# A hybrid attention encoder on one core: TensorE's queue written out in program order, with projections, scores and V products paced by TensorE time

## The chip, the cores and the metric

The program runs on one core of a Trainium2 chip. The metric is the device time of one execution in microseconds, the median over the runs; lower is better. The core has TensorE (matrix products into PSUM), VectorE, ScalarE, GpSimd, and the queue of SyncE, from which nearly all DMAs are issued. In rows they are PE (PEld is its weight loads), DVE, ACT, POOL and SP.

## What is computed

One layer of an encoder with two mixers, for a prompt of 2048 positions and a sample of 512, with the same weights:

```
h = rmsnorm(x, g_pre) * (1 + scale) + shift            # shift, scale, gate = Linear(silu(c))
qa, ka, va, ga, qb, kb, vb, gb = split(h @ w_in)       # 1024 -> 4096; rope on q and k
ya = dilated_mixture(qa, ka, va) * silu(ga)            # 8 heads, windows (128,1), (512,4), (2048,16)
yb = diff_attention(qb, kb, vb, lam, g_sub) * silu(gb) # 4 heads: (softmax_1 - lam * softmax_2) @ v, dense
x  = x + gate * rmsnorm(concat(ya, yb) @ w_out, g_post)
```

All products are made of fp16 pairs: a value is a high part plus a low part, and a product is three matrix products (high by high, high by low, low by high), summed in PSUM.

## The kernel before

The work is cut into eight groups of columns: four of B (one head each, g = 4 to 7) and four of A (two heads each, g = 0 to 3), taken in the order 4, 0, 5, 1, 6, 2, 7, 3. The rows are cut into five blocks of 512: four of the prompt (p, c = 0 to 3) and the sample (s). The loop runs over the groups and, in each, over the blocks. One turn of it has **attention** of this group and block (`items`) and **projections** for what comes next (`qg_proj`: Q and gate of the next block; `kv_proj`: K and V of the same block for the next group), and from the last group on also the **output projection** (`out_proj`).

An item of B (`ItemB`, 128 rows, two maps m = 0 and 1) makes scores in halves of 1024 columns: two matmuls at L615 and two at L621, the latter on 64 rows of the array. VectorE scales each half in place and takes its row minimum (L624), ScalarE makes the exponentials (L636), VectorE joins the two maps (L655), ScalarE and GpSimd split the result (L657, L665), DMA transposes bring it to the layout of the V product, and 48 matmuls at L679 make it (`tail2`). At j = 3 four transposes (L704) and an evacuation end a block. An item of A (`ItemA`, 32 positions of each of four residues) has eight matmuls of 32 columns of the array at L738 and eight at L744, two reductions at L751 and L753, an exponential (L758), a split (L772, L774), transposes by DMA, and for four items together V products at L793 and L799.

The attention is a software pipeline in `run_items`: while item n makes scores, the one before it is split (`tail1`) and an earlier one has its V product (`tail2`, `tail3`). The V product of B is made two items later, at the point "late", behind the second map; that of A at "mid", three items later (`p3`).

PSUM in the loop: three places "sc" of 1024 columns for scores, one place "pj" of 512 for projections, one "pv" for V products, the transposes of B and `gate_half`. K/V (L472, evacuated by L478, L487 and L488), Q (L546, L553) and gate (L569, L573, L574) all go through "pj".

What sets the order: the loop emits attention and projections interleaved by `interleave`, and the framework's scheduler then puts every engine's instructions in the order of a simulated run, by readiness and priority (`high_priority` puts an instruction earlier). So TensorE's queue follows the simulated run and not the text. Side work (weight scaling in `raw_scale` with a maximum that goes through DRAM, `allmax_slow`, L194; splitting of weights, gates of the output) is woven in between (`weave`). When the last group has finished a block, `y_scale` makes the scale for that block through `allmax_slow`, and only then can `y_first` load and split it for the output projection (L946).

## Time and profile before

| | |
|---|---|
| median of 3 runs | 2251.14 us (2244.3 to 2253.18) |
| profiled execution | 2248.76 us, of which the instructions span 2247.0 us |
| TensorE busy | 1924.8 us (86%), 18506 matmuls |
| VectorE busy | 1421.3 us (63%) |
| ScalarE busy | 1159.5 us (52%) |
| GpSimd busy | 727.7 us (32%) |
| mean granted TensorE clock | 0.936 of full speed |
| DMA | 360.99 MB, 71.4% of the 16 engines' time on the main queue |

The stages in what follows are called B0, A0, B1, A1, B2, A2, B3, A3 in the order of the groups; a stage is the stretch from its first score matmul to that of the next group. Before B0 lie 170.3 us of opening, behind A3's last V product the rest of the output projection. A row of a group of instructions has the line, engine, operation, what it writes and reads, shapes and count, then busy time and mean duration of one, then the engine's idle time before them with what ended it. In a row of the timeline, the start and the duration come first, and idle time before it stands in brackets. Matmuls overlap, so what one costs is read from start to start.

### The profile page before, as it was taken

Reading aid. Unit: us, or ns where it says so; the run is one execution under the profiler, and the core shown is the slowest. Engines: PE = TensorE matmul, PEld = TensorE weight load, DVE = VectorE, ACT = ScalarE, POOL = GpSimd, SP = SyncE. Lnnn points to the kernel's source line nnn. Section 1 sums busy time; section 2 is a strip of 40 time slices with the busy share of each in tenths; the row PEclk is TensorE's granted clock in tenths of the full one; section 3 lists DMA queues with packets and bytes.
Section 4 is the critical chain, followed back from the end, with each engine's and each line's share of the span. In section 5 each row is a group of like instructions: output and inputs, shape, how many; then the busy total and the mean of one; then the engine's idle time right before and its main releaser. Section 6 shows DMA issues by size and latency. Waiting matters only on the chain. (4 is left out here: it accounts for less than half of the span.)

```text
span 2247.0 us, 47773 instructions
## 1 busy us (share of the span) xinstructions
PE 1924.8 (86%) x18506; PEld 1283.8 (57%) x18506; DVE 1421.3 (63%) x3224; ACT 1159.5 (52%) x2361; POOL 727.7 (32%) x1299
## 2 busy tenths in 40 slices
PE   4788997889799978988799878987789886999998
PEld 2565665566656655766466556764556654444443
DVE  3766776755677876665677857666567745454543
ACT  4556675644457655544467646454466643333321
POOL 1234654411146653111266451112445530110000
PEclk7899999999999989999799989998889998999999
DMA  7585877879777887887378778789676769465453
GB/s 301 165 254 141 161 176 142 168 140 190 153 157 147 156 179 152 164 158 166 91 148 162 157 187 152 154 175 250 127 161 133 167 154 182 110 126 125 120 164 113
DMA packets 727667, 360.99 MB, mean 161 GB/s; under 512 B 640432, under 2 KB 687296, under 8 KB 723984
## 3 DMA queue, kind: packets, MB, share of 16 engines
q1 hardware_dynamic: 726608, 357.08, 71.4%
q8 instruction: 145, 2.38, 0.5%
q0 software_dynamic: 832, 0.86, 0.5%
q14 instruction: 82, 0.67, 0.1%
HBM read 165.64 MB, written 36.98 MB: 90 GB/s over the span
## 5 line engine op out<-in xcount | busy, mean ns | idle before, releaser
L472 PE MATMUL pj<-w,h 128*128 128x256 f16 x3840 | 481.7, 282 | 66.9 <-DVE Vs L488 27.3
L472 PEld LDWEIGHTS <-h 128*128 128x128 f16 x3840 | 378.4, 101 | 149.5 <-issue 83.0
L665 POOL TENSOR_TENSOR hl<-pp,hl 128x1024 f16<-128x1024 f32 (+1 forms) x144 | 291.8, 2043 | 109.4 <-ACT hl L657 105.8
L546 PE MATMUL pj<-w,h 128*128 128x128 f16 x3840 | 265.2, 224 | 20.0 <-ACT q L553 8.6
L455 POOL TENSOR_TENSOR rp<-q,tab_sb 128x64 f32<-128x64 f32 x160 | 64.3, 402 | 635.1 <-ACT q L478 375.3
L546 PEld LDWEIGHTS <-h 128*128 128x128 f16 x3840 | 231.3, 100 | 58.3 <-issue 49.0
L624 DVE TENSOR_SCALAR_CACHE_REDUCE sc<-sc,us 128x1024 f32<-128x1024 f32 (+1 forms) x160 | 188.4, 1179 | 75.3 <-PE sc L621 74.8
L569 PE MATMUL pj<-h,w 128*128 128x512 f16 x960 | 223.4, 386 | 12.6 <-ACT q L553 12.6
L615 PE MATMUL sc<-K,Qc 128*128 128x512 f16 x512 | 162.6, 399 | 76.0 <-ACT pp L636 67.0
L679 PEld LDWEIGHTS <-at 128*128 128x128 f16 x3264 | 199.2, 102 | 35.9 <-issue 19.8
L774 DVE SCALAR_TENSOR_TENSOR hl<-pp,Z,hl 128x640 f16<-128x640 f32 (+2 forms) x160 | 140.9, 886 | 112.9 <-DMA at<-hl 63.4
L624 DVE TENSOR_SCALAR_CACHE_REDUCE sc<-sc,us,nb 128x1024 f32<-128x1024 f32 x128 | 172.4, 1347 | 57.0 <-PE sc L621 38.2
L679 PE MATMUL pv<-V,at 128*128 128x128 f16 x3072 | 198.8, 227 | 9.5 <-DMA at<-hl 8.2
L636 ACT ACTIVATE pp<-sc,nb 128x1024 f32<-128x1024 f32 (+1 forms) x144 | 152.5, 1062 | 85.9 <-DVE sc L624 55.2
L758 ACT ACTIVATE pp<-pp,nb 128x640 f32<-128x640 f32 (+2 forms) x160 | 131.5, 822 | 125.2 <-DVE nb L753 116.0
L772 ACT ACTIVATE hl<-pp,Z 128x640 f16<-128x640 f32 (+2 forms) x160 | 129.6, 821 | 109.0 <-DMA at<-hl 89.1
L655 DVE SCALAR_TENSOR_TENSOR pp<-pp,rz,pp 128x1024 f32<-128x1024 f32 (+1 forms) x144 | 172.3, 1233 | 1.8
L657 ACT ACTIVATE hl<-pp 128x1024 f16<-128x1024 f32 (+1 forms) x144 | 141.5, 1002 | 46.0 <-DVE pp L655 43.6
L569 PEld LDWEIGHTS <-w 128*128 128x128 f16 x960 | 92.9, 99 | 125.5 <-issue 27.0
L946 PEld LDWEIGHTS <-w 128*128 128x128 f16 x960 | 92.5, 98 | 115.0 <-issue 13.7
L636 ACT ACTIVATE pp<-sc,nbs 128x1024 f32<-128x1024 f32 (+1 forms) x144 | 152.5, 1061 | 10.3 <-DVE pp L655 6.1
L751 DVE CUSTOM_DVE_ANT_0 pp<-sc,maskp,us 128x384 f32<-128x384 f32 (+1 forms) x128 | 85.8, 679 | 77.6 <-PE sc L744 77.3
(210 smaller groups left out, 3085.6 us busy)
## 6 DMA issues: line engine op xcount, KB each, us to landing
h<-hp SPq DMA_DIRECT2D x124, 512.0 KB, 6.3
pp<-in_x_p_dram SPq DMA_DIRECT2D x32, 512.0 KB, 5.3
raw<-in_w_in_dram SPq DMA_DIRECT2D x8, 2048.0 KB, 8.3
h<-hs SPq DMA_DIRECT2D x32, 512.0 KB, 6.2
out_dram<-pp SPq DMA_DIRECT2D x20, 512.0 KB, 3.0
at<-hl SPq DMA_TRANSPOSE x608, 3.2
hp<-h SPq DMA_DIRECT2D x4, 2048.0 KB, 12.4
yp<-yt SPq DMA_DIRECT2D x32, 256.0 KB, 2.8
```

The source lines that it names most:

```text
L472: mm(ps[:, jj, :], lhsT=hT[:, a, k, j * P:(j + 1) * P], rhs=w[:, k, b, :], start=(k == 0 and i == 0), stop=(k == KT - 1 and i == 2))
L546: mm(ps[:, jj, 0:128], lhsT=hT[:, a, k, j * P:(j + 1) * P], rhs=w[:, k, b, 0:128], start=(k == 0 and i == 0), stop=(k == KT - 1 and i == 2))
L569: mm(ps, lhsT=w[:, k, b, 128:256], rhs=hT[:, a, k, :], start=(k == 0 and i == 0), stop=(k == KT - 1 and i == 2))
L615: mm(ps[:, n * 512:(n + 1) * 512], lhsT=Qc[:, j, m, 0, :], rhs=K[:, t:t + 4, m, :], start=True, stop=False)
L624: V.tensor_scalar(ps[:, :HW], ps[:, :HW], u["nsc"], nb[:, 0:1] if hf else 3e38, op0=ALU.mult, op1=ALU.min, accum_out=nb[:, hf:hf + 1])
L636: act(pt[m, hf][:, :HW], pss[hf][:, :HW], AF.Exp, scale=-1.0, bias=nbs, accum_out=Z[:, 2 * m + hf:2 * m + hf + 1])
L655: V.scalar_tensor_tensor(a, a, rz[:, 1:2], pt[0, hf][:, :HW], op0=ALU.mult, op1=ALU.add)
L657: act(hi[:, :HW], a, AF.Copy)
L665: nc.gpsimd.tensor_tensor(lo[:, :HW], a, hi, op=ALU.subtract)
L679: mm(po[:, :128], lhsT=a[:, k, :], rhs=Vv[:, k, 128 * b:128 * b + 128], start=(k == 0 and i == 0), stop=(k == NT - 1 and i == 2))
L758: act(sb[:, :NA], sb[:, :NA], AF.Exp, scale=-1.0, bias=nb[:, 1:2], accum_out=Z[:, 0:1])
L774: V.scalar_tensor_tensor(lo[:, :NA], sb[:, :NA], rz, hi[:, :NA], op0=ALU.mult, op1=ALU.subtract)
```

## The change

- **Program order.** The loop runs under `manual_schedule` for TensorE: its queue takes the matmuls as the text emits them. The other engines are scheduled as before; evacuations and reductions that free a PSUM place get `high_priority(offset=EARLY)`, EARLY = 150.
- **Pacing.** `pace` takes the place of `interleave`: the fill (projections) goes on when its TensorE time is not above its share of the attention's, plus a lead that shrinks to none; all costs (`yield 0.75` and so on) are TensorE times. While there is one "pj" alone, a projection begins only after 3.0 us of attention since the last ended (GAP).
- **Places.** `proj_bank` lets projections alternate between "pj" and a score place in all A groups and in the sample's block, and once at a group's start. Transposes at the end of a B block and `gate_half` go to a score place too.
- **V products.** Those of B are halved: 24 matmuls at "mid", between the two maps, the rest at "late". Those of A come one item later (`p4`).
- **Output projection.** Its share in the last group's block 1 falls from 20 to 8 (OPC).

```diff
-LEAD = [0, 0, 0, 0]
-OPC = [0, 20, 24, 24, 30]
+LEAD = [1.0, 6.0]
+GAP = 3.0
+EARLY = 150
+OPC = [0, 8, 24, 24, 30]
...
+    def proj_bank():
+        t = BANK["last"] = "sc" if (BANK["turns"] or BANK["once"]) and BANK["last"] == "pj" else "pj"
+        BANK["once"] = False
+        return PT([P, PS["w"]], t)[:, 0:512] if t == "sc" else PT([P, 512], t)
...
-            ps = PT([P, 2, 256], "pj")
+            ps = proj_bank().rearrange("p (a b) -> p a b", a=2)
...
-            act(k32.rearrange("p a b d -> p a (b d)"), ps[:, :, 0:128], AF.Copy, scale=2.0 ** -19)
+            with tc.high_priority(offset=EARLY):
+                act(k32.rearrange("p a b d -> p a (b d)"), ps[:, :, 0:128], AF.Copy, scale=2.0 ** -19)
...
                     if k % 4 == 3:
-                        yield 0.23
+                        yield "half" if i == 1 and k == NT // 2 - 1 else 0.27
...
-                pt_ = PT([P, 4, P], "pv")
+                pt_ = PT([P, PS["w"]], "sc")[:, 0:512].rearrange("p (a b) -> p a b", a=4)
...
-            yield 0.53 * Cc / 512
+            yield 0.93 * Cc / 512
...
-            yield 0.22
+            yield 0.75
...
                 if x == "mid":
-                    for q in (p3, p2):
-                        if isinstance(q, ItemA) and not q.done and (q is p3 or not isinstance(it, ItemA)):
-                            yield from q.tail2(getattr(it, "last", None))
+                    for q in (p4, p3, p2):
+                        if isinstance(q, ItemA) and not q.done and (q is p4 or not isinstance(it, ItemA)):
+                            yield from q.tail2()
...
+                    if isinstance(p2, ItemB):
+                        rest = p2.tail2()
+                        for y in rest:
+                            if y == "half":
+                                yield 0.27
+                                break
+                            yield y
                 elif x == "late":
+                    yield from rest
                     if isinstance(p3, ItemB):
                         yield from p3.tail3()
-                    if isinstance(p2, ItemB):
-                        yield from p2.tail2(getattr(it, "last", None))
...
+    def pace(main, mcost, fill, fcost, lead):
+        m = f = 0.0
+        start = True
+        while main is not None or fill is not None:
+            wait = start and BANK["gap"] and not BANK["once"] and PACE["since"] < GAP
+            if fill is not None and not (wait and main is not None) and                     (main is None or f <= fcost * m / mcost + lead * max(0.0, 1.0 - m / mcost)):
+                x = next(fill, None)
...
-    for n, g in enumerate(ORDER):
+    with tc.manual_schedule(engines={mybir.EngineType.PE}):
+        for n, g in enumerate(ORDER):
...
+                BANK["turns"] = n + 1 < NU and (g < 4 or r == "s")
+                BANK["once"] = n + 1 < NU and i == 0
+                BANK["gap"] = n + 1 < NU and not BANK["turns"]
+                pace(main, mc, weave(chain(*fl), side, 5 if side.__name__ == "raw_split" else 2), fc, LEAD[i == 0])
```

The order of TensorE's queue moves in three places that matter here. In the first, an A group (A0, block 1), the scores of several items stood together before; the rows leave out the weight loads and the repeats of a row (sc is the score tile, K and Qc what it is made of, w, h and pj a projection, at and pv a V product):

```order
L738 MATMUL sc_6774<-K_1783,Qc_6049 32x512
...
L744 MATMUL sc_6774<-K_1783,Qc_6049 32x256
...
L738 MATMUL sc_6847<-K_1783,Qc_6049 32x512
...
L744 MATMUL sc_6847<-K_1783,Qc_6049 32x256
...
L793 MATMUL pv_6892<-at,V_1786 128x128
...
L472 MATMUL pj_6564<-w_3269,h_5397 128x256
```

The same stage now, block 1 (L760 was L738, L766 was L744, L561 was L546):

```order
L561 MATMUL sc_6043<-w_1574,h_5399 128x128
...
L760 MATMUL sc_6068<-K_1785,Qc_5410 32x512
...
L561 MATMUL sc_6043<-w_1574,h_5399 128x128
...
L766 MATMUL sc_6068<-K_1785,Qc_5410 32x256
...
L561 MATMUL sc_6043<-w_1574,h_5399 128x128
...
L760 MATMUL sc_6125<-K_1785,Qc_5410 32x512
```

Each run of eight score matmuls now stands by itself between pieces of projections, and the projections also write into score places. Counted over TensorE's queue, it passes from the 32-column matmuls to others or back 93, 63, 63 and 505 times in A0 to A3 before, and 153, 153, 153 and 141 times now.

The second place is A3, where before nearly every score matmul stood alone between others, with its weight load (block 2):

```order
L738 LDWEIGHTS Qc_26646
L738 MATMUL sc_27290<-K_22374,Qc_26646 32x512
L546 LDWEIGHTS h_26632
L546 MATMUL pj_27300<-w_21759,h_26632 128x128
L738 LDWEIGHTS Qc_26646
L738 MATMUL sc_27290<-K_22374,Qc_26646 32x512
```

In A3 now, from the end of block 0's V products to the first matmul of the output projection (L976, L946 before):

```order
L821 MATMUL pv_26883<-at,V_3927_26051 128x4x32
...
L585 MATMUL pj_26864<-h_26101,w_21797 128x512
...
L760 MATMUL sc_26967<-K_22376,Qc_26106 32x512
...
L766 MATMUL sc_26967<-K_22376,Qc_26106 32x256
...
L760 MATMUL sc_27004<-K_22376,Qc_26106 32x512
...
L976 MATMUL pj_27029<-raw_24742,w_27021 128x512
```

The runs of eight are whole again. Between block 0's last V product and the output projection stand 12 gate matmuls and three runs of scores. Of the 960 matmuls of the output projection, 480 stood ahead of the last V product before, and 432 do now.

The third place is the steady state of B0: before, one item's half of scores, the whole V product (48 matmuls), the next half:

```order
L615 MATMUL sc_2012<-K_443,Qc_676 128x512
...
L621 MATMUL sc_2012<-K_443,Qc_676 128x512
...
L679 MATMUL pv_2035<-V_444,at 128x128
...
L615 MATMUL sc_2123<-K_443,Qc_676 128x512
...
L621 MATMUL sc_2123<-K_443,Qc_676 128x512
...
L546 MATMUL pj_2647<-w_408,h_1776 128x128
```

In B0 now (L632, L638 and L697 were L615, L621 and L679; L485 was L472):

```order
L632 MATMUL sc_2851<-K_443,Qc_1793 128x512
...
L638 MATMUL sc_2851<-K_443,Qc_1793 128x512
...
L697 MATMUL pv_2865<-V_444,at 128x128
...
L485 MATMUL pj_2874<-w_1565,h_1778 128x256
...
L697 MATMUL pv_2865<-V_444,at 128x128
...
L632 MATMUL sc_2926<-K_443,Qc_1793 128x512
```

Both halves of the first map now stand together; between them and the second map lie 24 matmuls of a V product and 30 of a projection in this item, and in the items with Q projections 24 and 48.

## Rows read from the trace of the kernel before

**Rows 1.** Windows by stage: length, busy time of each engine, granted clock, DMA share.

```profile
170.30:416.00 245.70, 218.78 (x2087) 148.03 (x2086) 181.04 (x319) 155.75 (x326) 136.01 (x202) 0.95 0.75 157
416.00:620.20 204.20, 172.88 (x2151) 129.98 (x2151) 127.24 (x393) 104.59 (x214) 35.27 (x104) 0.95 0.81 162
620.20:872.10 251.90, 223.01 (x2185) 151.47 (x2183) 187.11 (x343) 158.81 (x336) 144.00 (x212) 0.96 0.75 156
872.10:1068.20 196.10, 169.36 (x2125) 130.51 (x2124) 118.34 (x359) 98.92 (x197) 28.56 (x90) 0.95 0.81 166
1068.20:1340.30 272.10, 230.71 (x2184) 156.78 (x2184) 196.30 (x360) 160.52 (x339) 143.72 (x214) 0.91 0.70 144
1340.30:1534.00 193.70, 168.04 (x2125) 129.53 (x2124) 117.84 (x357) 98.95 (x197) 27.32 (x92) 0.96 0.82 169
1534.00:1829.30 295.30, 245.44 (x2234) 166.08 (x2234) 199.37 (x347) 166.15 (x347) 141.63 (x214) 0.88 0.76 165
1829.30:2134.00 304.70, 276.00 (x2005) 134.00 (x2005) 150.25 (x409) 110.36 (x209) 25.82 (x64) 0.95 0.61 134
```

**Rows 2.** Waits over the whole span: who waited for whom, total us, times, longest.

```profile
DVE amc L194 <- DMA amr<-amd: 109.4, 13, 12.6
...
PE sc L615 <- ACT pp L636: 71.3, 49, 12.1
...
PE pv L793 <- DMA at<-hl: 50.2, 23, 16.5
...
PE pj L472 <- DVE Vs L488: 27.3, 7, 11.2
...
PE pj L472 <- DVE V L488: 21.9, 10, 9.6
```

**Rows 3.** Groups of A1 (872.10 to 1068.20), the three kinds of projections on TensorE.

```profile
L472 PE MATMUL pj<-w,h 128*128 128x256 f16 x480 | 59.3, 283 | 4.5 <-DVE V L488 2.6 <-DVE Vs L488 1.9
L546 PE MATMUL pj<-w,h 128*128 128x128 f16 x480 | 29.3, 219 | 0.9 <-ACT q L553 0.9
L569 PE MATMUL pj<-h,w 128*128 128x512 f16 x121 | 27.2, 379 | 1.2 <-ACT q L553 1.2
```

**Rows 4.** Chain of work that ended last: its last long piece, the output projection alone.

```profile
2135.52 103.61 PE pj L946 x480
```

**Rows 5.** Timeline of TensorE in A3: scores and Q projection one by one.

```profile
1930.51 0.39 PE L738 MATMUL sc<-K,Qc 128*32 128x512 f16 x1
1930.84 0.23 PE L546 MATMUL pj<-w,h 128*128 128x128 f16 x1
1931.00 0.39 PE L738 MATMUL sc<-K,Qc 128*32 128x512 f16 x1
```

**Rows 6.** Timeline of TensorE in A3: runs of eight scores with a projection behind.

```profile
1868.39 0.62 PE L738 MATMUL sc<-K,Qc 128*32 128x512 f16 x8
1868.83 0.39 PE L744 MATMUL sc<-K,Qc 128*32 128x256 f16 x8
1869.16 0.45 PE L546 MATMUL pj<-w,h 128*128 128x128 f16 x5
1869.54 0.61 PE L738 MATMUL sc<-K,Qc 128*32 128x512 f16 x6
```

**Rows 7.** Timeline of TensorE in A3 around the first output projection.

```profile
1881.27 1.06 PE L799 MATMUL pv<-at,V 128*128 128x128 f16 x16
...
1900.73 3.59 PE L793 MATMUL pv<-at,V 128*128 128x128 f16 x32 [16.48 <-DMA at<-hl]
...
1905.96 0.90 PE L946 MATMUL pj<-raw,w 128*128 128x512 f16 x2
```

**Rows 8.** Groups of B1 (620.20 to 872.10) on VectorE and ScalarE.

```profile
L624 DVE TENSOR_SCALAR_CACHE_REDUCE sc<-sc,us,nb 128x1024 f32<-128x1024 f32 x32 | 43.1, 1348 | 11.7 <-PE sc L621 6.3 <-ACT pp L636 4.8 <-issue 0.4
L655 DVE SCALAR_TENSOR_TENSOR pp<-pp,rz,pp 128x1024 f32<-128x1024 f32 x32 | 40.2, 1296 | 0.3
L636 ACT ACTIVATE pp<-sc,nb 128x1024 f32<-128x1024 f32 x32 | 35.4, 1110 | 20.8 <-DVE E L171 9.2 <-DVE sc L624 8.9 <-DVE us L337 2.7
```

More of the change, by code (lines that the diff above doesn't have):

```diff
@@ L975, in call, with weave, interleave @@
         yield 0.0
-    def weave(a, b, off=OFF[1]):
+    def weave(a, b, every=1):
+        n = 0
         for x in a:
             yield x
-            with tc.high_priority(offset=off):
-                x = next(b, 0.0)
-            yield x
-        while True:
-            with tc.high_priority(offset=off):
-                x = next(b, None)
-            if x is None:
-                return
-            yield x
-    def interleave(main, mcost, fill, fcost, lead=0):
+            n += 1
+            if n % every == 0:
+                yield next(b, 0.0)
+        yield from b
+    def interleave(main, mcost, fill, fcost):
         m = f = 0.0
@@ L999, in interleave @@
             m += cst
-            while not done and f / fcost < (m - lead) / mcost:
+            while not done and f / fcost < m / mcost:
                 try:
@@ L1006, in interleave @@
             run(fill)
+    PACE = {"since": 9.0}
+    def pace(main, mcost, fill, fcost, lead):
[5 more added lines that the diff above has]
+                x = next(fill, None)
+                if x is None:
+                    fill = None
+                    continue
+                f += x
+                if x == 0.05:
+                    start = True
+                    PACE["since"] = 0.0
+                elif x:
+                    start = False
+            elif main is not None:
+                with tc.high_priority(offset=OFF[0]):
+                    x = next(main, None)
+                if x is None:
+                    main = None
+                    continue
+                m += x
+                PACE["since"] += x
     assert NSB["s"] == 1
```

232 lines of the change are left out of this document (124 added, 108 removed).

## The prediction

> **What bounds the kernel now.** I read the table of stages first, because a share over the whole span mixes four kinds of stage. In it one is to look at the length of a stage beside TensorE's busy time, and then at the other engines and at DMA. [rows 1] TensorE is the busiest engine in every stage. Its idle time is length less busy time: in B0 to B3 it is 26.9, 28.9, 41.4 and 49.9 us, together 147.1; in A0 to A2 it is 31.3, 26.7 and 25.7, together 83.7; in A3 it is 28.7. So the loop (170.3 to 2134 us) holds some 260 us of idle TensorE. That is the most that a better order could return, were TensorE's busy time to stay what it is.
>
> It will not stay, and this is the second thing to see in the same table: A3 is busy for 276.0 us, with fewer matmuls (2005) than A1 (2125, 169.4 us). [rows 1] A3 has no K/V projection and one block less of Q and gate, and it has 480 output matmuls instead. By A1's groups it should be busy for 169.4 - 59.3 (K/V) - 29.3/5 - 27.2/5 (a fifth of Q and gate) + 103.6 (480 matmuls of the output projection, at the pace of the stretch where they run alone) = 202.4 us. [rows 1, 3, 4] The other **73.6 us** need a cause, and the timeline has it: a score matmul and a Q matmul alternate, each by itself, with steps of 0.33 and 0.16 us from start to start. [rows 5] In a run of eight, the same score matmul takes 0.44/8 = 0.055 us, since four of 32 columns run beside each other; a Q matmul in a row takes about a quarter of the output matmul's 103.61/480 = 0.216 us, so 0.054. [rows 4, 6] A pair costs 0.49 us alone and 0.11 in company.
>
> The waits say what ends TensorE's idle time: exponentials that hold the score places (71.3 us in 49 waits), DMA transposes ahead of A's V products (50.2), and evacuations of the single "pj" place by L488 (27.3 and 21.9). VectorE itself waits 109.4 us, 13 times, for the maximum that goes through DRAM. [rows 2]
>
> **The change, part by part.** *A3, single matmuls.* Program order makes all scores runs of eight: the passes between score matmuls and others fall from 505 to 141, and A1's busy time, from which 202.4 was built, already holds 63. A pass is not free. Five Q matmuls take 0.38 us from their start to the next scores, 0.11 more than five times 0.054; a run of eight at 256 columns takes 0.33 us up to the next Q matmul, against half of 0.44 = 0.22 in company. [rows 6] So a pass costs about 0.1 us in either direction, and 78 more passes give back 8 us: -73.6 + 8 = -66.
>
> *A3, the first output product.* It needs the scale of block 0. From the end of that block's V product to the first output matmul passed 1905.96 - 1882.33 = 23.6 us, and TensorE stood idle for 16.48 of them. [rows 7] Program order now puts behind that V product 12 gate matmuls (2.6 us by 0.216 each) and three runs of scores (1.7 us with their passes), then the output matmul, whose chain I leave as long. The hole becomes 23.6 - 4.3 = 19.3 us, +3. The 48 output matmuls that leave the loop run behind it at 0.216 us, the pace they should have in it: nothing in the sum. A3 in all: **-63**.
>
> *A0 to A2.* Two of the three waits lose their cause: a projection has a second place, so L488 can be late by a whole projection, and the V product comes an item later, so the transposes have more time. The wait for Q's transposes is left. I take half of the 83.7 us: -42. Against it stand passes: 60 more in A0 and 90 more in each of A1 and A2, 240 by 0.1 = +24. Sum: **-18**.
>
> The trace bears on the price of a pass from two sides. The lower one is 0.1. The upper one is the pair of singles: two passes for 0.38 us, 0.19 each, though that holds the lost company as well. [rows 5, 6] I take 0.1, because runs of eight are what the new order has. The Trainium skill (TensorEngine Tiling (Array Packing), section Tiling Modes) says that a change of tiling mode drains TensorE, which speaks against this part of the change; the rows agree that a pass costs something, and the full drain is a rival below.
>
> *B0 to B3.* Scores, exponentials and V products stay what they are, as does the number of passes to 64-row matmuls; what moves is what lies between the maps. The second map needs a score place that the first exponential sets free. By rows: from the end of the first map's second half VectorE needs 1.35 us and its read-out, ScalarE the scaled minimum and 1.11 us of exponential. [rows 8] I estimate 3.9 us for that chain with VectorE's first half still running at its start. In the new order lie a half V product (24 by about 0.056 = 1.3 us), 30 K/V matmuls (3.2 us at 0.108, half of an output matmul's 0.216) and one half of scores (about four by 0.216): about 5 us, so there is a cover with about 1 us to spare. Of the 147.1 us idle I leave the share of the maximum through DRAM, five waits in these stages at the mean of 109.4/13 = 8.4 us, 42 us: the change only spreads that work. [rows 1, 2] Half of the other 105 goes, -52: the ends of the stages, where projections of the sample's block hold "pj" one after another, get the second place, and steady state has its cover; the other half stays because VectorE is busy 187 of 252 us and, in a stage as long as TensorE's 223 us, would be busy 84%. B2 and B3 had a clock of 0.91 and 0.88 against 0.96 in B1, and 7.7 and 22.4 us more TensorE time; B3 has 49 more matmuls. [rows 1] Less idling should bring back a quarter, -8. Sum: **-60**, bounds 0 and -125.
>
> *At nothing:* the higher priority of evacuations moves work on VectorE and ScalarE without adding any. SP's and GpSimd's queues get the same DMAs; a transpose of A's has its reader an item later, while its buffer is free an item less, two items ahead of the next writer. `gate_half` and B's transposes take a score place for one evacuation each. If VectorE were late, these would be the first to hold a map back.
>
> The sum is -63 - 18 - 60 = **-141 us**. Against the profiled execution, 2248.8 us, it gives 2107.7; the median of the runs is 2.4 us higher, so I say **2110 us**.
>
> **The rivals.** *The idle time only moves.* B is held by VectorE and ScalarE (187 and 159 us of 252), and A by DMA, whose engines are busy 0.81 of 196 us = 159, against TensorE's 169. [rows 1] Then only A3 gains, 63, and the passes cost 24: 39 us, **2212**. For it: 84% load in VectorE leaves little slack for a queue that cannot pass a wait. Against it: TensorE's waits for L488 come of one place, not of a busy VectorE.
>
> *A pass is a full drain.* As a mechanism here: at a pass the next matmul starts only when the last has left the array, which is its duration of 0.23 us less its step of about 0.056, so 0.17. [rows 5] A0 to A2 pay 41 instead of 24, A3 13 instead of 8: -63 becomes -58, -18 becomes -1, the total -119, **2132**. The rows so far show 0.1, so it is unlikely. It is the rule named above, taken to its end.
>
> *Slower: the second map waits in a queue that cannot go round it.* With program order nothing else runs on TensorE while the second map stands at its score place. The place is VectorE's: if the two joins of L655 (2 by 1.30 = 2.6 us) stand ahead of the reductions of the first map, the exponential comes 2.6 us late; 1 us is covered, and each of the 64 prompt items of B waits 1.6 us: +102. [rows 8] Instead of -60, that gives -63 - 18 + 102 = +21, **2272**. It is slower than before as soon as the mean added wait of an item passes 81/64 = 1.3 us. For it: 49 such waits already. Against it: reductions and exponentials now have the higher priority.
>
> *More than I take.* B reaches its lower bound (-125), and all of the idle time of A0 to A2 goes (-84 + 24): -248, **2003**.
>
> **How the numbers follow.** Forecast 0.50, idle moved 0.18, drain 0.08, slower 0.16, more 0.08. About 0.5% (11 us) is what a measurement of this kernel can tell from no change. Of "idle moved" 0.04 and of "slower" 0.03 fall within it: faster 0.80, same 0.07, slower 0.13. The range is 2035 to 2235: it holds the forecast, "drain" and "idle moved", and leaves out "slower" and most of "more". The forecast's own range is 2060 to 2160.
>
> **What would show it.** A3's busy time near 210 us with no alternating singles; one hole of about 19 us ahead of the first output product; A0 to A2 about 190 us long, busy for more than before and idle for less, no wait for L488 above a few us; B0 to B3 near 230, 235, 255 and 280 us, the waits for exponentials halved. It is wrong if A3 stays above 280 us, if scores of B wait over 1.3 us per item, or if A stages get longer.

## The result and the profile after

The changed kernel takes 2187.0 us (median of 4 runs, 2184.56 to 2200.39), the kernel before 2247.72 us beside it (4 runs, 2243.72 to 2253.18): 0.974 of it, 95% interval 0.969 to 0.979. That is 61 us less where 141 were forecast: within the range, the right sign, less than half of the size. The profiled execution took 2184.56 us, its span is 2182.8 us; the span before was 2247.0, so 64.2 us are to be accounted for.

The table of stages now, which answers to [rows 1]: length, then busy time of TensorE, its weight loads, VectorE, ScalarE and GpSimd, then granted clock, DMA share and GB/s. The last two lines are A3 up to the end of its last V product, and the rest of the output projection.

```profile
171.40:422.90 251.50, 220.96 (x2216) 153.29 (x2217) 190.40 (x334) 159.50 (x336) 141.53 (x216) 0.97 0.75 154
422.90:613.50 190.60, 170.57 (x2078) 113.60 (x2078) 124.39 (x374) 100.39 (x199) 26.61 (x89) 0.96 0.88 170
613.50:871.90 258.40, 222.35 (x2235) 154.54 (x2232) 196.64 (x344) 160.32 (x338) 136.71 (x215) 0.96 0.74 153
871.90:1060.60 188.70, 170.45 (x2078) 113.73 (x2077) 124.53 (x374) 99.81 (x198) 28.03 (x90) 0.96 0.87 171
1060.60:1320.30 259.70, 226.98 (x2236) 156.39 (x2233) 195.27 (x344) 160.83 (x338) 136.89 (x216) 0.94 0.74 152
1320.30:1510.40 190.10, 171.58 (x2079) 114.02 (x2078) 118.77 (x356) 97.91 (x194) 27.52 (x90) 0.96 0.88 175
1510.40:1801.20 290.80, 238.41 (x2288) 162.77 (x2289) 203.84 (x348) 168.04 (x351) 142.48 (x218) 0.92 0.79 172
...
1801.20:2060.80 259.60, 202.36 (x1885) 99.08 (x1885) 146.63 (x405) 106.19 (x203) 24.31 (x58) 0.90 0.75 146
2060.80:2182.80 122.00, 114.12 (x528) 51.55 (x527) 47.74 (x78) 24.97 (x54) 9.99 (x26) 0.98 0.44 136
```

Against [rows 1], with A3 and the rest of the output projection taken together ("tail"; before, A3's last V product ends at 2135.52 us, where [rows 4] starts):

| us | before | after | moved | forecast |
|---|---|---|---|---|
| B0 to B3, length | 1065.0 | 1060.4 | -4.6 | -60 |
| their idle time of TensorE | 147.1 | 151.7 | +4.6 | -52 |
| A0 to A2, length | 594.0 | 569.4 | -24.6 | -18 |
| their idle time | 83.7 | 56.8 | -26.9 | -42 |
| A3 and tail, length | 417.7 | 381.6 | -36.1 | -63 |
| opening | 170.3 | 171.4 | +1.1 | 0 |

Two things in this table are not gains or losses of the new order. Work changed its stage: the Q projections (L546, now L561) have 240 matmuls more in B0 to B3 than before (2112 against 1872), 144 fewer in A0 to A2 and 96 fewer in A3. At 0.054 us each that is some 13 us into B, 8 out of A0 to A2 and 5 out of A3. And the granted clock of B2 and B3 rose from 0.91 and 0.88 to 0.94 and 0.92: TensorE's busy time in B fell by 9.2 us although B has that much more to do.

The waits of TensorE after, as in [rows 2] (total us, times, longest), and VectorE's wait for the maximum that goes through DRAM:

```profile
PE sc L632 <- ACT pp L656: 77.6, 34, 7.9
PE pv L815 <- DMA at<-hl: 43.3, 25, 7.5
PE pv L697 <- ACT o L710: 32.1, 31, 3.6
PE sc L760 <- DVE nb L776: 31.7, 12, 12.1
PE pj L976 <- ACT w L952: 21.0, 1, 21.0
PE pv L697 <- DMA at<-hl: 14.5, 10, 3.7
...
PE pj L485 <- DVE Vs L503: 12.8, 4, 4.7
PE pj L485 <- DVE V L503: 9.0, 8, 1.3
```

```profile
DVE amc L196 <- DMA amr<-amd: 105.0, 13, 12.4
```

The waits for L488 (now L503) went from 49.2 to 21.8 us, the number of waits for exponentials from 49 to 34, their sum from 71.3 to 77.6. One wait is new: a V product of B waits 32.1 us for the evacuation of the one before. One has grown: scores of A wait 31.7 us for VectorE, 28.9 of them in A3, where all groups together had 5.8 us before.

**A3 lost its singles.** The timeline shows runs of eight scores (0.55 and 0.33 us up to the next instruction) with twelve Q matmuls between them, where [rows 5] had one and one:

```profile
1824.05 0.61 PE L760 MATMUL sc<-K,Qc 128*32 128x512 f16 x8
1824.60 0.84 PE L561 MATMUL pj<-w,h 128*128 128x128 f16 x12
1825.37 0.40 PE L766 MATMUL sc<-K,Qc 128*32 128x256 f16 x8
1825.70 0.84 PE L561 MATMUL pj<-w,h 128*128 128x128 f16 x12
1826.48 0.62 PE L760 MATMUL sc<-K,Qc 128*32 128x512 f16 x8
```

Its idle time is twice what it was, 57.2 against 28.8 us. (In this last group PSUM is cut otherwise than the section on the kernel says, before and after: two places for scores, three for projections.) TensorE stands before the first output product, the hole of [rows 7], and three times later at scores that wait for VectorE (7.1, 12.1 and 8.2 us), as here:

```profile
1866.02 1.03 PE L976 MATMUL pj<-raw,w 128*128 128x512 f16 x2 [20.97 <-ACT w L952]
...
1925.37 1.04 PE L760 MATMUL sc<-K,Qc 128*32 128x512 f16 x8 [7.05 <-DVE nb L776]
```

VectorE's timeline says why it was late at 1925: its queue stood at the maximum of block 1, and the score reductions lie behind it. The other two gaps lie behind such reads too, of 10.97 and 9.71 us.

```profile
1923.02 0.29 DVE L196 TENSOR_REDUCE amc<-amr 128x1 f32<-128x128 f32 x1 [10.48 <-DMA amr<-amd]
```

**B's large gaps lie at the same events as before.** The timeline of VectorE in B1, after: eight weight maxima in a row, then the read of their maximum, each ahead of score reductions (L642).

```profile
805.12 4.83 DVE L308 TENSOR_REDUCE mg<-raw 128x1 f32<-128x512 f32 x8
...
827.34 0.29 DVE L196 TENSOR_REDUCE amc<-amr 128x1 f32<-128x128 f32 x1 [10.11 <-DMA amr<-amd]
...
828.30 1.28 DVE L642 TENSOR_SCALAR_CACHE_REDUCE sc<-sc,us 128x1024 f32<-128x1024 f32 x1
```

TensorE waits behind both:

```profile
812.27 4.17 PE L485 MATMUL pj<-w,h 128*128 128x256 f16 x24 [3.27 <-DVE Vs L503]
...
832.49 0.59 PE L632 MATMUL sc<-Ks,Qc 128*128 128x512 f16 x1 [7.94 <-ACT pp L656]
```

The kernel before, at the same read in B1, VectorE and TensorE:

```profile
826.79 0.29 DVE L194 TENSOR_REDUCE amc<-amr 128x1 f32<-128x128 f32 x1 [9.87 <-DMA amr<-amd]
...
828.54 0.42 DVE L488 SCALAR_TENSOR_TENSOR Vs<-pj,Vs 128x256 f16<-128x256 f32 x1
```

```profile
829.01 4.43 PE L472 MATMUL pj<-w,h 128*128 128x256 f16 x20 [8.51 <-DVE Vs L488]
```

So two of the three longest waits "for L488" of [rows 2], this one and that of 11.2 us in B2, were VectorE standing in that read, with the evacuation queued behind it. In the third, 9.6 us in A0, VectorE and ScalarE stood 8.5 us for DMA transposes. A second place lets the matmuls behind L488 pass, and TensorE stops at its next score place instead: waits for exponentials ahead of the sample's scores (Ks), three of them right behind such a read, rose from 4.3 us in 2 waits to 23.1 in 4; ahead of the prompt's they fell from 67.1 us in 47 to 54.5 in 30.

**A0 to A2 wait for other things.** The waits of A1, before and then after (all over 2 us):

```profile
PE pv L793 <- DMA at<-hl: 7.3, 6, 2.7
PE sc L738 <- DMA Qc<-tq: 5.2, 3, 2.9
PE pv L793 <- issue: 2.8, 1, 2.8
PE pj L472 <- DVE V L488: 2.6, 3, 1.4
```

```profile
PE pv L815 <- DMA at<-hl: 15.0, 7, 6.1
PE pv L697 <- DMA at<-hl: 3.0, 1, 3.0
```

Over A0 to A2, waits for L488 went from 19.8 us to 2.1 and those for Q's transposes from 11.9 to none, but those of A's V products for their transposes rose from 28.0 to 40.3.

### The profile page after: what moved, and what is told of

Read it like the earlier page. It is cut to its first block, busy times and chain, and to the rows that moved or that the text cites. A ratio compares the mean times of both kernels' runs of the same rounds, so it can differ in the third digit from the quotient of the medians.

```text
span 2182.8 us, 47915 instructions
## 1 busy us (share of the span) xinstructions
PE 1856.9 (85%) x18506; PEld 1211.3 (55%) x18506; DVE 1449.8 (66%) x3224; ACT 1163.1 (53%) x2361; POOL 710.5 (33%) x1299
## 5 line engine op out<-in xcount | busy, mean ns | idle before, releaser
L485 PEld LDWEIGHTS <-h 128*128 128x128 f16 x3840 | 362.1, 101 | 136.9 <-issue 51.8
L485 PE MATMUL pj<-w,h 128*128 128x256 f16 x2928 | 390.2, 280 | 31.3 <-DVE Vs L503 12.8
L697 PEld LDWEIGHTS <-at 128*128 128x128 f16 x3264 | 213.5, 99 | 90.7 <-issue 49.5
L697 PE MATMUL pv<-V,at 128*128 128x128 f16 x3072 | 231.2, 222 | 31.5 <-ACT o L710 26.7
L642 DVE TENSOR_SCALAR_CACHE_REDUCE sc<-sc,us 128x1024 f32<-128x1024 f32 (+1 forms) x160 | 189.0, 1181 | 95.7 <-PE sc L638 95.4
L561 PEld LDWEIGHTS <-h 128*128 128x128 f16 x3840 | 224.1, 99 | 38.0 <-issue 33.7
L632 PE MATMUL sc<-K,Qc 128*128 128x512 f16 x512 | 156.6, 388 | 59.9 <-ACT pp L656 54.5
L642 DVE TENSOR_SCALAR_CACHE_REDUCE sc<-sc,us,nb 128x1024 f32<-128x1024 f32 x128 | 172.6, 1348 | 28.0 <-PE sc L638 22.2
L585 PE MATMUL pj<-h,w 128*128 128x512 f16 x720 | 189.8, 393 | 1.0 <-ACT q L569 1.0
L561 PE MATMUL pj<-w,h 128*128 128x128 f16 x2736 | 175.7, 222 | 10.5 <-DVE wS L120 7.1
L675 DVE SCALAR_TENSOR_TENSOR pp<-pp,rz,pp 128x1024 f32<-128x1024 f32 (+1 forms) x144 | 172.2, 1230 | 2.0
L976 PEld LDWEIGHTS <-w 128*128 128x128 f16 x960 | 90.6, 99 | 132.6 <-ACT w L952 21.5
L585 PEld LDWEIGHTS <-w 128*128 128x128 f16 x960 | 84.2, 101 | 91.7 <-issue 32.6
L976 PE MATMUL pj<-raw,w 128*128 128x512 f16 x480 | 115.4, 387 | 21.5 <-ACT w L952 21.0
```

The source lines that it names most:

```text
L485: mm(ps[:, jj, :], lhsT=hT[:, a, k, j * P:(j + 1) * P], rhs=w[:, k, b, :], start=(k == 0 and i == 0), stop=(k == KT - 1 and i == 2))
L561: mm(ps[:, jj, 0:128], lhsT=hT[:, a, k, j * P:(j + 1) * P], rhs=w[:, k, b, 0:128], start=(k == 0 and i == 0), stop=(k == KT - 1 and i == 2))
L585: mm(ps, lhsT=w[:, k, b, 128:256], rhs=hT[:, a, k, :], start=(k == 0 and i == 0), stop=(k == KT - 1 and i == 2))
L632: mm(ps[:, n * 512:(n + 1) * 512], lhsT=Qc[:, j, m, 0, :], rhs=K[:, t:t + 4, m, :], start=True, stop=False)
L642: V.tensor_scalar(ps[:, :HW], ps[:, :HW], u["nsc"], nb[:, 0:1] if hf else 3e38, op0=ALU.mult, op1=ALU.min, accum_out=nb[:, hf:hf + 1])
L675: V.scalar_tensor_tensor(a, a, rz[:, 1:2], pt[0, hf][:, :HW], op0=ALU.mult, op1=ALU.add)
```

## The experiments

**Theory:** what is left of B's idle time hangs on stalls in VectorE's queue and on chains from scores to exponentials, which an order of TensorE's queue can move but not remove; A3 gave back part of its gain at VectorE's reads. **Rivals:** the halved V products or the priorities cost B what the rest gains; VectorE is simply too busy; A3 is held by its transposes.

The runs were made in four batches, and runs of a batch share the times of the kernel before; its median was 2262.6 us (e1 to e6), 2265.7 (e4, e10, e2), 2262.5 (e11, e12, c2, c3) and 2262.8 (the last three). All times there are some 0.7% longer than in the first comparison, so totals are compared by ratio. Each stage length is that of one profiled execution. A yardstick for B are e4_amc_y, which leaves B as changed, and e10_pvbank, whose edit there had no effect: 1073.6 and 1073.0 us. In e2_early0, which changes priorities alone, B took 1065.5, so differences under some 10 us in B say little. A3 + tail lies between 384 and 393 us in nine kernels whose A3 is as changed (at 381.6 in the first comparison and at 399.9 in e1_whole), so differences under 10 us there say nothing. Not in the table is the opening: 164 to 166 us in the five kernels with pinned side work (e11_side and the four with c), 173 to 179 in the other ten. Why was not followed; some 9 us of what these five gain belong to no stage of the argument.

| run | median us | ratio to before, 95% | B0 to B3 | A0 to A2 | A3 + tail |
|---|---|---|---|---|---|
| the change | 2187.0 | 0.974 (0.969 to 0.979) | 1060.4 | 569.4 | 381.6 |
| e1_whole | 2317.1 | 1.022 (1.019 to 1.025) | 1171.2 | 573.1 | 399.9 |
| e3_pj | 2262.6 | 0.999 (0.997 to 1.002) | 1101.7 | 595.8 | 383.8 |
| e6_a_only | 2224.0 | 0.982 (0.979 to 0.985) | 1077.8 | 569.0 | 392.5 |
| e6_a3_only | 2432.4 | 1.074 (1.071 to 1.076) | 1068.9 | 792.6 | 392.3 |
| e4_amc_b | 2191.6 | 0.968 (0.965 to 0.971) | 1057.5 | 574.9 | 391.5 |
| e4_amc_y | 2191.3 | 0.967 (0.964 to 0.970) | 1073.6 | 571.0 | 364.9 |
| e10_pvbank | 2209.0 | 0.975 (0.972 to 0.977) | 1073.0 | 574.7 | 386.7 |
| e2_early0 | 2203.9 | 0.973 (0.971 to 0.976) | 1065.5 | 570.4 | 389.4 |
| e11_side | 2175.9 | 0.963 (0.959 to 0.967) | 1037.1 | 580.1 | 387.6 |
| e12_join | 2191.1 | 0.969 (0.965 to 0.974) | 1059.3 | 570.8 | 384.8 |
| c3_both | 2154.8 | 0.954 (0.949 to 0.958) | 1031.4 | 581.6 | 374.0 |
| c2_prefetch | 2136.7 | 0.945 (0.941 to 0.949) | 1031.8 | 580.1 | 360.1 |
| e13_vearly | 2255.4 | 0.997 (0.995 to 0.999) | 1137.4 | 562.7 | 385.8 |
| c4_pins | 2158.3 | 0.953 (0.950 to 0.955) | 1033.4 | 599.8 | 363.3 |
| c5_vearly_pins | 2240.7 | 0.989 (0.985 to 0.992) | 1116.6 | 600.3 | 361.5 |

**e1_whole: the V product of B whole again.**

```diff
+                elif x == "late":
                     if isinstance(p2, ItemB):
-                        rest = p2.tail2()
-                        for y in rest:
-                            if y == "half":
-                                yield 0.27
-                                break
-                            yield y
-                elif x == "late":
-                    yield from rest
+                        for y in p2.tail2():
+                            yield 0.27 if y == "half" else y
```

> The changed kernel with the V products of B made whole at the late point again; all else, program order included, as changed. Theory (B's idle time is set by the evacuation chains on ScalarE and VectorE, and an order of TensorE's queue only moves it): the 32 us that TensorE waits at the V place for the previous product's evacuation (L697 <- ACT o) fall below 5, the second maps wait about as much more at their score places, sum of B0 to B3 within 12 us of 1060.4, total 2175 to 2200. Rival 1 (the halving is itself the loss, since a product begun early only adds a wait for the one V place): the 32 us are gained, 2150 to 2165. Rival 2 (the halving is the cover that the prediction took it for, 1.3 us of 5 against a chain of 3.9 us): 64 items wait 0.2 us or more longer, 2200 or above.

The wait at the V place fell from 32.1 to 8.8 us, not quite as far as the theory had it, but the exponentials took far more than it gave:

```profile
PE sc L632 <- ACT pp L656: 186.2, 65, 10.6
...
PE pv L697 <- ACT o L710: 8.8, 4, 5.6
```

B is 98 us longer than the yardstick, 1.5 us for each of the 64 prompt items; the lost cover (the matmuls that stand in the queue while an exponential is made) is half a V product, 1.3 us. Of the 98 us, 69 are idle time, 1.1 us an item. The other 29 are busy time for the same matmuls: the granted clock of the four B stages was 0.92, 0.92, 0.93 and 0.90, against 0.97, 0.94, 0.94 and 0.92 in e4_amc_y. Rival 2 is right, with far more than its 0.2 us an item. Program order without the halving makes the kernel 2.2% slower than before, near the size of the prediction's slower rival (+102). That one gave another cause (joins ahead of reductions) and no lower clock, so that the sizes agree is in part luck.

**e3_pj: no projection in a score place.** `turns` and `once` are set to False. As `gap` is set where `turns` is not, the 3.0 us of attention ahead of each projection now hold in A groups and the sample's block as well: the run takes the second place away and holds projections back, and what each costs cannot be told apart.

> The changed kernel with every projection in the one place pj, none in a score place. The step of the prediction (the second place is what takes L488's waits out of A): A0 to A2 have 20 to 30 us more idle time, all of it ahead of K/V matmuls, total 2205 to 2220. Rival (program order spreads projections between scores, so one place is enough): A0 to A2 within 8 us of 569.4, total 2182 to 2195. Theory for B: the sample's block and the start of a group have only pj, some 5 us more per group at the most.

Nothing of the change's gain is left: the ratio is 0.999, at 2262.6 us where at most 2220 were expected. A0 to A2 have 92.3 us of idle time against 56.8, and are 25 us longer than in e4_amc_y (8 of them are 144 Q matmuls that stay there). K/V matmuls, which waited for nothing, now wait 24.3 us, 19.9 of them for the gate's evacuation (L591) and 4.4 for L503. So one place is too few, as the prediction's step has it, but "all of it ahead of K/V matmuls" is not so. B is 28 us longer, where at most 20 were expected; its longest wait, 12.4 us, is a V product waiting for L710.

**e6_a_only and e6_a3_only: program order in some groups alone.**

```diff
-    with tc.manual_schedule(engines={mybir.EngineType.PE}):
+    with nullcontext():
...
+                with tc.manual_schedule(engines={mybir.EngineType.PE}) if g < 4 else nullcontext():
+                    pace(main, mc, ...)
```

(e6_a3_only: `if g2 is None`.)

> The changed kernel with program order on TensorE in the A groups alone; in the B groups the scheduler orders TensorE's queue again, the text being the changed one (halved V products, pacing, places, priorities). Theory (order on TensorE does not bind B): B0 to B3 sum to 1050 to 1072 as with program order, A3 and A0 to A2 as with it, total 2177 to 2199. Rival 1 (program order pins V products and second maps in B and costs it what places and priorities gain): B 15 to 40 us shorter, total 2147 to 2172. Rival 2 (the prediction's step: program order gives B its cover): B longer by 20 us or more, total above 2207.

> The changed kernel with program order on TensorE in the last group (A3) alone, the scheduler elsewhere. Theory: A3 as in the changed kernel (about 260 us to its last V product, busy near 207); A0 to A2 lose their 24.6 us of gain, since the scheduler again bunches scores and projections; B as with e6_a_only; total 20 to 30 us above e6_a_only, so 2197 to 2229. Rival (A0 to A2 gained from the later V product and the second place, not from the order): within 8 us of e6_a_only.

With the scheduler in B the total is 0.8% above the change, some 18 us and at rival 2's bound, but the stages don't bear that rival out: B is 4 us above the yardstick, the opening 4 us longer than in e1_whole and e3_pj, and A3 + tail, where the order is the same, at the upper end of its spread. So program order with halving is worth little in B, and rival 1 is out. What differs is the name of the idle time: B's V products now wait for their transposes (14.5 us with program order), and next to nothing waits for exponentials (77.6):

```profile
PE pv L697 <- DMA at<-hl: 85.0, 54, 4.5
...
PE sc L632 <- ACT pp L656: 5.4, 11, 1.9
```

e6_a3_only went as nobody expected: A0 to A2 take 792.6 us with no idle time at all. Out of the changed text the scheduler makes in every A stage what it made in A3 before:

```profile
1040.20 0.28 PE L766 MATMUL sc<-K,Qc 128*32 128x256 f16 x1
1040.42 0.28 PE L485 MATMUL pj<-w,h 128*128 128x256 f16 x1
1040.63 0.28 PE L766 MATMUL sc<-K,Qc 128*32 128x256 f16 x1
1040.84 0.28 PE L485 MATMUL pj<-w,h 128*128 128x256 f16 x1
```

Each step is 0.215 us. TensorE's busy time of that stage is 263.3 us against 170.5 after, at a granted clock of 1.00 against 0.96. The queue passes between score matmuls and others 759 times in it, against 153. So "busier" was slower here: without program order, the changed text makes each A stage some 74 us longer.

**e4_amc_b and e4_amc_y: the read of a maximum later in VectorE's queue.** The reduction at L196 is put behind the latest score reduction that the text has come to; e4_amc_b does it for weights, six side steps after the DMAs, e4_amc_y for the scales of y.

```diff
+        row = allmax_slow(ag) if n else None
+        for _ in range(LATER if n else 0):
+            yield 0.0
...
+        with tc.issue_after(LAST["v"]) if behind and LAST["v"] is not None else ExitStack():
+            V.reduce_max(m, row, axis=AX.X)
...
+        return (r, c) in YS or ((r, c) in YR and PACE["t"] - YR[r, c][1] > AGE)
```

> The changed kernel with VectorE's read of the weights' maximum (L196, the row that has gone through DRAM) put some ten score reductions later in VectorE's queue, for raw_scale and wo_scale; nothing else moved. Theory (B's idle time that is left comes of side work on VectorE standing ahead of score reductions, which an order of TensorE's queue cannot pass): the four gaps of 6.0, 7.9, 7.0 and 6.9 us ahead of L632 at these reads go, B0 to B3 shorter by 18 to 30 us in sum, total 0.8 to 1.4% below the changed kernel's ratio of 0.974. Rival (the second maps would have waited there for another reason, since VectorE is busy for 190 of 255 us anyway): the gap only moves, sum of B within 8 us of 1060.4, ratio 0.970 to 0.978.

> The changed kernel with y_scale cut in two: its DMAs at once, VectorE's read of the maximum only after 12 us more of paced TensorE time, and y_first waiting for that. Only A3 and the tail can change. Theory (A3's gain was given back because VectorE stands in the read while TensorE, in program order, stands at a score matmul with output matmuls behind it): the hole of 21.0 us ahead of the first output product and the three gaps of 7.1, 12.1 and 8.2 us go; A3 and tail together shorter by 25 to 45 us, ratio 0.954 to 0.963. Rival (A3 is held by its DMA transposes and VectorE's hl chain, 0.74 and 150 us of 264): the idle time comes back as waits at L815 and L760, gain under 12 us, ratio above 0.968.

e4_amc_b: the waits for exponentials fell from 77.6 to 47.8 us, B is 16 us below the yardstick, the ratio 0.6% lower. That is between theory and rival: much of the 30 us came back as waits of V products (for the place 44.0 us after 32.1, for transposes 26.3 after 14.5). e4_amc_y: the three gaps of 7.1, 12.1 and 8.2 us are gone and A3 + tail is 17 us below the change and 19 or more below the nine kernels above, ratio 0.967; less than expected, because the hole ahead of the first output product stayed (18.7 us).

**e10_pvbank and e2_early0.** The first makes `po` a column slice of one tile for four items (`st["po"][:, j, :]`), the second sets EARLY to 0.

> The changed kernel with the four V products of a B block side by side in one allocation of the V place (128 columns each), so that three of four need not wait for the evacuation of the one before. Theory (the halved V product brought this wait in): L697 <- ACT o falls from 32.1 us to under 10; half or more of it comes back as waits for exponentials at the next score matmul, since the product is ahead of a map that is no earlier; B shorter by 5 to 16 us, ratio 0.966 to 0.972. Rival 1 (all of it is real): B shorter by 22 us or more, ratio 0.964 or less. Rival 2 (it was cover for the exponentials all along): within 4 us.

> The changed kernel without the higher priority of evacuations and reductions (EARLY = 0). The prediction put this at nothing by itself but relied on it against the second map's wait. Theory: joins and splits stand ahead of reductions more often; L632 <- ACT pp rises from 77.6 to 110 us or more, B longer by 20 to 60 us, ratio 0.983 to 1.001. Rival (the scheduler's readiness order is nearly the same without it): within 10 us, ratio 0.970 to 0.979.

e10_pvbank did not do what it was made for: the V product (L699 there) still waited 31.3 us, 31 times, for the evacuation, so it says nothing on the price of that wait. e2_early0 is within the rival's bounds (waits for exponentials 78.4 us): the priorities are worth nothing that these runs can tell. The prediction had them at nothing, but leaned on them against its slower rival.

**e11_side: side work pinned between reductions.** Each maximum and split of weights goes behind the latest score reduction (VectorE) or exponential (ScalarE) of the text, by the same `issue_after`.

> e4_amc_b, and beside the read of the maximum all side work on weights (the eight maxima at L308, the splits at L328 and L329) pinned behind the latest score reduction or exponential of the text, so that they stand one by one between reductions instead of four or eight in a row. Theory (side work ahead of reductions is what holds B): the gaps of 3.2 and 4.2 us near the end of each B stage go, sum of B 8 to 20 us below e4_amc_b's 1057.5, ratio 0.959 to 0.965. Rival (TensorE waits there for the single V place or the end of the block, whatever stands on VectorE): within 6 us, ratio 0.965 to 0.971.

B is 20 us below e4_amc_b, the far end of the theory, and the two stalls near the end of B0, B1 and B2 went. With e4_amc_b, 36 of B's 1073 us were side work standing ahead of reductions. The opening gave another 10 us, which nobody expected.

**e12_join: less work on VectorE.** L675 works on `[:, :HW // 2]`.

> The changed kernel with the join of the two maps (L675) made on half its columns, which leaves out half of that sum and takes some 20 us off VectorE in each B stage (195 to 175 of 255 us). Theory (VectorE's load, with its queue, sets what is left of idle time in B): sum of B 25 to 60 us shorter, ratio 0.947 to 0.963. Rival 1 (B's idle time hangs on single stalls and on the chain scores, minimum, exponential, not on VectorE's load): sum of B within 12 us, ratio 0.968 to 0.976.

The run leaves out half of that sum. VectorE's busy time in B1 fell from 196.64 to 175.75 us; TensorE's idle time there is 36.4 us, after 36.1. Over B, idle time is 151.3 us, as in the change (151.7) and 8 to 10 below the yardstick (159.4 and 160.8), and B is some 14 us below it, the ratio 0.969: rival 1, or a little over its bound. So VectorE's load is worth 14 us of B at the most, not the 25 to 60 of the theory.

**c3_both and c2_prefetch: the gains together.** c2_prefetch also emits `y_first` as soon as the scale is read, and its matmuls 8 us of paced time later.

```diff
-            while nxt is None:
-                if y_made[r, c] == NU:
-                    nxt = y_first(r, c, j)
...
+            while OP["nxt"] is None or (PACE["t"] < 1e6 and PACE["t"] - OP["t"] < HOLD):
+                prefetch()
```

> e11_side and e4_amc_y in one. If their gains lie in different stages, they add: 0.967 times e11_side's ratio by 0.974, about 0.950 to 0.958. If they are the same idle time seen twice, no better than the better of the two.

> c3_both, and the load and split of the first rows for the output projection (y_first) emitted as soon as the scale is read, its matmuls 8 us of paced TensorE time later. Theory (the hole of 18.7 us ahead of the first output product is the chain read, load, split, with nothing left to run in program order): it falls to 3 us or less, A3 and tail 10 to 18 us shorter than c3_both. Rival (the output matmuls that come later are missed in block 1, where TensorE then waits for score places): less than 5 us.

The gains add: 0.954, then 0.945. In c2_prefetch the first output matmul follows gate and scores without a gap, and A3 + tail is 14 us shorter than in c3_both:

```profile
1854.65 2.12 PE L606 MATMUL pj<-h,w 128*128 128x512 f16 x9
1856.69 0.40 PE L787 MATMUL sc<-K,Qc 128*32 128x256 f16 x8
1857.03 1.25 PE L1017 MATMUL pj<-raw,w 128*128 128x512 f16 x5
```

c2_prefetch, 2136.7 us, beats both kernels: 0.945 of before, some 3% below the change.

**e13_vearly, c4_pins, c5_vearly_pins: what is left in B.** e13_vearly moves the second half of the V product:

```diff
                     yield 0.52 * (HW // 512)
+                    if m == 1 and hf == 0 and NH == 2:
+                        yield "late0"
...
+                elif x == "late0":
+                    yield from rest
```

> The changed kernel with the second half of B's V product ahead of the second map's second half of scores instead of behind it, so that its evacuation can be asked for 0.9 us of TensorE time (and two exponentials of ScalarE) sooner. Theory (the wait for the V place, 32 us, is real idle time): L697 <- ACT o falls below 15 us, B 10 to 25 us shorter, ratio 0.963 to 0.970. Rival (the half product was cover for nothing and the second half of scores, now later by 1.3 us, delays its exponential and the next item's first map): B the same or longer, ratio 0.973 to 0.985.

> c2_prefetch, with wo_scale's eight maxima (1.2 us each, on weights that come by DMA) pinned behind score reductions too, and with the pinned side work of A groups left to the scheduler again. Theory (B3's idle time is wo_scale's maxima ahead of reductions, and pins only cost in A, where VectorE is not late): B3 10 to 20 us shorter than 288.9, A0 to A2 5 to 10 us shorter than 580.1, ratio 0.932 to 0.939. Rival (B3's idle time comes from the gate's products and their places): B3 within 5 us, ratio 0.940 to 0.946.

> c4_pins and e13_vearly in one. If the V place and side work are separate causes, their gains add: c4_pins' ratio less 0.4 to 1.1%. If e13_vearly is no gain, the same as c4_pins or above it.

e13_vearly: the wait at the V place falls as in e1_whole, and the exponentials take more than twice as much again.

```profile
PE sc L632 <- ACT pp L658: 131.0, 58, 4.8
PE pv L699 <- ACT o L712: 8.8, 5, 2.6
```

B is 64 us longer, 1 us an item, the rival by far. Only 26 of the 64 are idle time; 38 are busy time at a lower granted clock (0.94, 0.91, 0.91 and 0.89 in the four stages). c5_vearly_pins repeats it on the better kernel (+83 us in B against c4_pins, 69 of them idle time). c4_pins refutes both its guesses: B3 is 294.0 us, no shorter, so wo_scale's maxima are not what holds it; and A0 to A2 got 20 us longer without the pins: the last V products of B (L718 there), which an A stage begins with, wait up to 10.0 us for their transposes, 28 us in the three stages against 5 in c2_prefetch. Why pins help in A was not followed further.

## Why the prediction was off

**The step that failed is B's:** "half of the other 105 goes, -52". B's idle time rose by 4.6 us instead, and B is 4.6 us shorter where 60 were forecast, or some 18 with the Q matmuls that came in counted off. The small term beside it, the clock's -8, came. The step rested on two readings. The first was wrong, the second left half of the matter out.

*The waits for places.* The prediction took the waits for L488 as waits of one place, and set the reads of the maximum aside as 42 us of their own. The timeline of the kernel before, shown above, has them as one event in the largest cases: 8.51 us "for L488" are VectorE's 9.87 us in the read. (VectorE stood 53.6 us in the five reads of B, not 42.) A new place does not remove such a stall, it hands it to the next wait: the waits for L488 fell by 27 us over the whole span, those ahead of the sample's scores rose by 19. Moving the reads and the side work itself was worth 36 us in B (e4_amc_b, e11_side); of gaps over 2.5 us, B had 94.7 us before (19 gaps), 83.5 after (18) and 43.9 in c2_prefetch (10).

*The cover with "about 1 us to spare".* The prediction priced the stretch between an item's two maps, and not the one from the second map to the next item's first. The one that it priced came out about as it said: its own terms leave 5.4 less 3.9, so 1.5 us to spare, and half of B's second maps had 1.85 us or more. With three score places that go round in turn for four halves an item, a half needs the place of the half three before it (all 30 waits for exponentials ahead of the prompt's scores end with that one's). So at the first boundary the second map's second half waits for the exponential of the first map's first half, which is what was priced, and at the second boundary the next item's second half waits for that of the second map's first half. In the change, 17 waits of the first kind took 27.1 us, and 10 of the second 26.8. After the second map, TensorE and ScalarE in B1:

```profile
713.10 0.39 PE L638 MATMUL sc<-K,Qc 64*128 64x512 f16 x2
...
714.97 1.28 PE L697 MATMUL pv<-V,at 128*128 128x128 f16 x20
716.08 0.59 PE L632 MATMUL sc<-K,Qc 128*128 128x512 f16 x2
716.61 0.39 PE L638 MATMUL sc<-K,Qc 64*128 64x512 f16 x2
716.93 0.60 PE L632 MATMUL sc<-K,Qc 128*128 128x512 f16 x2
```

```profile
715.05 1.11 ACT L656 ACTIVATE pp<-sc,nb 128x1024 f32<-128x1024 f32 x1 [2.16 <-DVE sc L642]
```

The next map's first half starts at 716.08 us in a place that has long been free. Its second half starts at 716.93, and the exponential that frees its place ends at 715.05 + 1.11 = 716.16, so there is 0.8 us to spare here. Of the 60 such starts in B's prompt blocks, 41 have less than 1.3 us, and half have 1.0 or less. Hence taking 1.3 us of cover away from the first boundary makes 52 of 64 second maps wait, 160.7 us in all (e1_whole), and taking it from the second makes 46 of 60 first maps wait, 104.1 us (e13_vearly), though both shorten the wait at the V place (from 32.1 to 8.8 us). The halving bought back what program order alone would have lost, and little more.

**A3: mechanism and main term right, -36 instead of -63.** Busy time went from 276.0 us [rows 1], 277.4 with the 1.5 us up to 2135.52, to 202.36 us; 48 output matmuls of 0.216 us left it for the tail and 96 Q matmuls (5 us) for the stage before, so the singles gave some 59 us, where 66 were forecast. The hole is 20.97 us, forecast 19.3. What is missing beside are the three gaps of 7.1, 12.1 and 8.2 us, together 27: scores pinned ahead of output matmuls, VectorE in the read of a maximum. The prediction asked what a late VectorE holds up in B, and did not ask it for the scales in A3. e4_amc_y takes these gaps away, and 17 us of A3 + tail with them.

**A0 to A2: right in sum (-24.6 for -18, and -17 without the Q matmuls that left), both terms too large, and the sum in part luck.** Idle time fell by 27 instead of 42 us. Of the three waits that the prediction named, L488's went as it said. The transposes ahead of V products were to have more time, and their waits rose by 12 us; those for Q's transposes were to stay, and went, 12 us. Why the V products wait longer, made an item later, was not followed. Busy time rose by 2.3 us; with the 144 Q matmuls that left for B, that is 10 us for 240 passes, 0.04 each, against 0.1 forecast. e3_pj, with 51 passes a stage, gives 0.055 by the same sum. In A3 the runs above still show 0.1 us a pass (twelve Q matmuls take 0.77 us where 12 by 0.054 are 0.65), so what offsets it in A0 to A2 stays open. The rival with a full drain, 0.17 us, is out. The Trainium skill's drain at a change of tiling mode (TensorEngine Tiling (Array Packing), section Tiling Modes) costs some 0.1 us here at most.

**What stays open:** c2_prefetch still has 126 us of idle time in B, 49 of it in B3, most in waits for exponentials (61.0 us) and at the V place (34.5). That the second is cover for the first is shown by e1_whole and e13_vearly. What a fourth score place would give was not tried, and what holds B3 is not known.

## What to carry to other kernels

A wait names who came last, not why: before a new buffer is credited with removing it, look at what stood ahead of the evacuation in that engine's queue. In a queue that cannot go round a wait, every boundary of the pipeline that needs a place needs its own cover, so count places against halves at each boundary. And a read of something that travels through DRAM belongs well behind its DMAs in the queue of an engine that others wait for: moving such reads and the side work around them, with the earlier load for the output projection (c2_prefetch), gave about as much again as the change itself. Last, a stage can get shorter because its work went into its neighbour, so count the matmuls of a stage before its length is read as a gain.

## What the runs showed of the hardware

Matmuls on 32 columns alternating one by one with matmuls on 128 columns took 0.215 us each, whatever kind, at a granted clock of 1.00 and with TensorE busy throughout (e6_a3_only), while runs of eight of the same score matmuls take 0.33/8 = 0.04 us each up to the next instruction (A3 of the changed kernel). A stage can thus be 100% busy and 75 us longer than one that idles for 18 us (A1: 263.3 against 188.7). Stages with the same matmuls and more idle time were busy for longer at a lower granted clock: 912.8 us in B of e4_amc_y, 941.9 in e1_whole and 951.1 in e13_vearly, with clocks of 0.92 to 0.97, 0.90 to 0.93 and 0.89 to 0.94. So a wait in most items cost more here than its idle time. And 20 us less work on VectorE a stage (e12_join) changed TensorE's idle time in B1 by 0.3 us.
